# Sample scores in a decoder layer: four transposes and copies first, then four products

## The chip, the cores and the metric

The kernel runs on one core of a Trainium2 chip. The metric is the device time of one execution in microseconds (us), as the median of several. PE is the TensorE engine (matrix products and transposes by a product with the identity), PEld its weight loads, DVE is VectorE, ACT is ScalarE, POOL is GpSimd, and SP issues most DMAs. PE and PEld run side by side. Each engine works through its own queue in a fixed order and waits where an instruction needs something that is not there yet.

## The reference: what matters of it

One layer of a decoder: a projection, sparse attention in three branches beside a state-space layer, an output projection and a feed-forward network, for 1024 prompt tokens and for 8 sample batches of 4 tokens each. The change is in the attention of the samples. Each batch has 32 query rows (4 tokens, 8 heads); the cached keys come from a window of 512 positions and from 2048 paged positions.

```python
full_s = jnp.concatenate([cache_kv_slc[l, page_table].reshape(row_shape), kv_s], axis=1)
win = jnp.concatenate([cache_kv_win[l], kv_w], axis=1)
...
s_s = jnp.einsum('bqgrd,bqgkjd->bqgrkj', qg, k_sel).reshape(bn, nq, N_KV, GQA, n_sel)
p_s = masked_softmax(s_s * scale, key_pos <= q_pos[None, :, None, None, None])
...
s_w = jnp.einsum('bqgrd,bwgd->bqgrw', qg, kv_win[:, :, 0]) * scale
```

## The kernel before

The samples are worked on in two halves of four batches. A half has five runs of 512 cached keys for each batch: one run of the window (branch 2) and four runs of the paged cache (branch 1). Names read `s`, branch, batch, run: `s102kT` are the turned keys of branch 1, batch 0, run 2. The first half has batches 0 to 3, the second 4 to 7.

`sample_scores` (L801) makes the scores of a run for the four batches of a half. For each batch `sample_keys` (L815) does three steps: four transposes on PE of the raw keys `s_raw` into one PSUM bank `kt` (L820; the tag `t` has two banks, so that the third batch needs the bank of the first), a copy of 128x512 numbers from that bank to `kT` in SBUF on ACT (L822), and a product of the 32 query columns `qblk` with `kT` into the batch's 32 rows of the bank `ss` (L823). Before, batch i's product stands in the code between the copy of batch i and the transposes of batch i+1. Then DVE masks the scores to `s_S` (L742, L747), takes their maximum (L752), ACT takes the exponential (L753), and `sample_pv` (L825) turns the weights (`pt`) and multiplies them with the values (L840, tile names that end in `o`, such as `s011o`). Behind that, `sample_load` gathers the rows of the run after next (L404, an indirect DMA that POOL issues); it writes into the buffers which that product has read, so the gather waits for it.

The order of the code is not the order of the queues. The program is built with a scheduler (`schedule_with_timeline_sim=True`) that gives every engine's queue its final order and mixes independent strands. Beside the first half's runs stand the compression of the paged keys (`compress`: `craw` gathered, `cxr` copied on ACT at L487, `ct` transposed at L494, split into `cXh` on ACT and `cXl` on DVE at L498 and L499, products `cp` at L516) and a scan of 128 steps on DVE (`ssm_scan`, L1526 to L1529, four small instructions in a chain for each step). Beside the second half's runs stand the first tiles of the prompt's attention: queries turned (`aqt`, `aqA`, `aqB`), scores `as` (L1195, L1196, L1199), maxima `asm` on DVE (L1203, L1211), exponentials `ap` on ACT (L1212), weights turned (`pt`, L1269) and copied (L1271), values `aso` (L1273), and the rest of the scan. The state-space outputs `Y` (L1601) that need the scan come later.

Of the kernel before, what the change touches and what calls it, by code (L numbers as in the profile page):

```python
# [20 lines left out]
D = 1024  # L21
NT = 8          # tiles of 128 prompt tokens
NK = 8          # tiles of 128 input features
# [5 lines left out]
def shape_constants():  # L29
    """Constants that depend on shapes and positions alone, packed as [128, n] columns."""  # L30
# [27 lines left out]
    # sample rows are (batch in the half, token, group, head in the group)  # L58
# [31 lines left out]
class Kernel:  # L90
# [35 lines left out]
    def psum(self, name, **tags):  # L126
        self.pp = self.open(name, space=PS)
        self.pbufs = tags
        self.tags = "to"
        for t in tags:      # the banks go to the tags in this order  # L130
            self.pp.tile([128, 512 * (2 if t == "s" else 1)], F32, tag=t, name=f"{name}_{t}", bufs=tags[t])
# [23 lines left out]
    def load_constants(self, ea):  # L155
# [26 lines left out]
        nc.vector.tensor_scalar(self.gain_q, self.gain_q, 0.125, None, op0=ALU.mult)     # with the scores' scale  # L182
        # vectors over features, turned to feature-major: b_ada 48, norm_mix_g 8, norm_ffn_g 8, attn_out_g 4, ssm_out_g 4
# [12 lines left out]
    # ---- 1/sqrt(x * a + b), elementwise, on a small tile: a guess from the exponent, scaled by c, and three of Newton's  # L196
    # steps without their factor of -1/2, so that the scale turns c into -2 c^3, three times, and ends at one ----
    def rsqrt(self, x, a, b, name, eng=None, tag="", pool=None, bufs=3):
# [5 lines left out]
        # the guess: the bits of (magic - half of the bits) with c in its exponent and sign  # L204
        V.tensor_scalar(y.bitcast(I32), s.bitcast(I32), -0.5, float(0x5F3759DF) + math.log2(-c) * 2 ** 23 - 2 ** 31, op0=ALU.mult, op1=ALU.add)
        for _ in range(3):
            V.tensor_tensor(t, y, y, op=ALU.mult)
            V.tensor_tensor(t, t, s, op=ALU.mult)
            if eng:     # only the vector engine does both at once
                V.tensor_scalar(t, t, 3.0 * c * c, None, op0=ALU.subtract)  # L210
                V.tensor_tensor(y, t, y, op=ALU.mult)
            else:
                V.scalar_tensor_tensor(y, t, 3.0 * c * c, y, op0=ALU.subtract, op1=ALU.mult)
# [18 lines left out]
    def ada_features(self, nb, ev, out):  # L232
        """out [128 feature, 4, 9] for the four 128-feature blocks, with the bias."""
# [8 lines left out]
    def ada_rows(self, nb, ev, pool, dst):  # L242
        """the nine rows, with the bias, to DRAM."""
# [34 lines left out]
    def phase_project(self):  # L278
        self.psum("psa", s=2, t=3, o=1)
        self.adaT = self.cst.tile([128, 4, 8, 9], F32, name="adaT")   # shift1, (1 + scale1) gain, and the FFN's  # L280
# [92 lines left out]
    def prep_c(self, pa):  # L373
        """silu of the nine conditions, feature-major; they come as rows (row, k-tile) of 128."""
# [26 lines left out]
    def gather(self, out, cache, b, j):  # L401
        """four positions of each of the 128 16-position chunks of a batch's paged rows: [128, 1024]."""
# [4 lines left out]
    def split(self, raw, hi, lo):  # L407
        """raw = hi + lo, each of twelve bits."""
# [3 lines left out]
    def compress_weights(self, pa, pb):  # L412
# [4 lines left out]
        for i, s in enumerate("kv"):  # L417
# [16 lines left out]
            # the encodings' part of the hidden layer: products summed over the positions, then over the partitions  # L434
# [13 lines left out]
    def compress(self, b, cp):  # L448
        """the compressed keys and values of a paged batch (the ninth is the prompt), four positions of each chunk at a
        time; the products of one part follow the turning of the next, and the output's product comes later still."""  # L450
# [23 lines left out]
    def c_turn(self, b, j, cp):  # L474
        """four positions turned and split, two positions times 64 on the partitions: [(hi, lo)] of keys and values."""
# [27 lines left out]
    def c_product(self, b, j, X, cp):  # L503
        """their part of the hidden layer, for the blocks that begin and the blocks that end with the chunk."""
# [51 lines left out]
    def gelu2(self, out, x, t):  # L556
        """twice the tanh form of gelu: x (1 + tanh(sqrt(2 / pi) (x + 0.044715 x^3))); t is scratch."""
# [7 lines left out]
    def sigmoid2(self, out, z):  # L565
        """twice the sigmoid: 1 + tanh(z / 2)."""
# [31 lines left out]
    def sample_modulate(self, xn, out, iscale, ishift, p):  # L598
        """xn [32, 1024] normalised rows to feature-major modulated out [128, 8, 32]."""
# [10 lines left out]
    def sample_qkv(self, ea, sa):  # L610
# [20 lines left out]
        # gates, as rows (b, t, g, r) of three  # L631
# [7 lines left out]
        # queries, block-diagonal over the two groups  # L639
# [22 lines left out]
    def sample_attend(self, half, sb):  # L662
        """a half of the sample batches; rows (batch, token, group, head). The keys come in runs of 512 cached ones
        (the last run of a branch has the new ones behind it), each with its own maximum; the runs are weighed at the end. It goes in seven steps,
        the second half's between the products of the prompt's attention."""
# [7 lines left out]
        # compressed branch  # L673
# [15 lines left out]
        # importance of the 30 blocks that are not forced, the ranks, the mask of those not among the best 13  # L689
# [27 lines left out]
        # the new keys' scores, of both other branches  # L717
# [42 lines left out]
        # weights of the runs: exp(their maximum - the largest) gate / sum; M holds the maxima negated  # L760
# [19 lines left out]
    def sample_begin(self, sb):  # L780
        """the runs of both halves; their rows are loaded two runs ahead."""
# [19 lines left out]
    def sample_scores(self, run, sb):  # L801
        half, br, j = run
        p = self.ps(self.XT[0], f"ss{half}{br}{j}")
        for i, raw in enumerate(self.raws[run]):
            b = 4 * half + i
            self.sample_keys(raw, b, p[32 * i:32 * i + 32, :], sb, i, f"s{br}{b}{j}")
        return p

    def own_group(self, out, O):
        """the own group's half of O [128 row, (g, d)]."""  # L810
# [4 lines left out]
    def sample_keys(self, raw, b, out, sb, i, name):  # L815
        """scores of the batch's 32 rows against four positions of each chunk: out [32, (l, chunk)]."""
# [5 lines left out]
        nc.scalar.copy(kT, p)  # L822
        nc.tensor.matmul(out, self.qblk[:, b, :], kT, start=True, stop=True)  # L823
# [22 lines left out]
    def modulated(self, xn, hi, lo, ishift, iscale, pool, name, tag="mod_h", bufs=2, banks=None, halves=(0, 1)):  # L846
        """normalised rows xn [128, 1024] of one prompt tile (or a half of them) to modulated feature-major hi and lo."""
# [15 lines left out]
    def prompt_rows(self, tt, xp, after=None):  # L863
        """a tile of the prompt, its rows over their root mean square."""
        nc = self.nc
        x = xp.tile([128, 1024], F32, tag="bx", name=f"bx{tt}")
        if after is not None:     # the modulation's weights come first
# [14 lines left out]
    def project_weights(self, nm, col, n, after=None):  # L882
        """n columns of the projection's weights, by halves of the features: as they are, and in high and low parts."""
# [14 lines left out]
    def project(self, cw, first):  # L898
# [9 lines left out]
        if 1:  # L908
            for kind, i, col, n in blocks:
# [7 lines left out]
                for t2 in range(NT // 2):  # L917
# [11 lines left out]
                    if kind == "u":  # L929
                        if nm == "u1" and t2 == 3:      # what follows in place of pb doesn't wait for it  # L930
# [18 lines left out]
            # gates  # L949
# [31 lines left out]
    def kv_turn(self, br, t2, kn, pb):  # L981
        """the keys split, high and low parts stacked over the partitions."""
# [12 lines left out]
    # ---- phase 3: the prompt's attention; between its products the state-space outputs and their gating, the rest of the  # L995
# [893 lines left out]
```

## Time and profile before

| | us |
|---|---|
| median of three executions | 1857.84 |
| the three executions | 1857.84, 1870.40, 1857.72 |
| span of the profiled execution | 1867.2 |
| PE busy in that span | 1779.7 (95%) |
| DVE, ACT, POOL busy | 953.9, 632.4, 423.4 |

The page of the profile tells the span of its execution and not the time around it. Of the three times only 1870.40 lies above that span, by 3.2 us. The other two are 12.6 us shorter than 1870.40.

### The profile page before, as it was taken

How to read it: one execution, taken by the hardware profiler on the slowest of the kernel's cores; microseconds unless marked ns; L12 is line 12 of the kernel's file. 1: busy time of each engine (PE TensorE's matmuls, PEld its weight loads, DVE VectorE, ACT ScalarE, POOL GpSimd, SP SyncE). 2: the span in 40 equal slices, each digit the busy share in tenths (PEclk: the TensorE clock that was granted, in tenths of full speed). 3: DMA queues.
4: the chain of work that ended last, by engine and by line, in shares of the span. 5: the costliest groups of instructions: out<-in, count | busy, mean ns of one | idle time of the engine just before them, and what ended most of it. 6: DMA issues, size and time to landing. Idle time of an engine off the chain costs nothing.

```text
span 1867.2 us, 29377 instructions
## 1 busy us (share of the span) xinstructions
PE 1779.7 (95%) x11546; PEld 1476.4 (79%) x11546; DVE 953.9 (51%) x2330; ACT 632.4 (34%) x1263; POOL 423.4 (23%) x817
## 2 busy tenths in 40 slices
PE   6898999899898999999989989999999999999997
PEld 3788998777655676565658889999999999999996
DVE  4867657667978433655755452332332332332346
ACT  4422146455555342565643341211211211211210
POOL 2334645232025310333112210100100100100140
PEclk9999999999899886999999999999999999999999
DMA  8333244544141111544225331201201201201113
GB/s 290 103 83 111 73 141 125 214 149 157 58 142 66 27 37 31 174 158 155 87 91 178 102 113 46 68 23 46 68 23 46 68 23 46 68 23 46 51 46 139
DMA packets 132700, 172.44 MB, mean 92 GB/s; under 512 B 17177, under 2 KB 92313, under 8 KB 132305
## 3 DMA queue, kind: packets, MB, share of 16 engines
q1 hardware_dynamic: 123024, 136.62, 23.0%
q0 software_dynamic: 9408, 33.89, 5.7%
q8 instruction: 91, 1.49, 0.3%
q14 instruction: 49, 0.39, 0.1%
q10 hardware_dynamic: 128, 0.04, 0.0%
HBM read 143.88 MB, written 25.46 MB: 91 GB/s over the span
## 4 chain that ended last, share of the span: by engine, by line
PE 83%; DVE 8%; DMA 4%; ACT 3%; issue 2%; POOL 0%; SPq 0%; another core or an unknown queue 0%; DVEq 0%; ACTq 0%; POOLq 0%
PE gu L1793 18%; PE dn L1836 13%; PE g L1793 5%; PE u L1793 4%; PE cp L516 4%; PE aso L1273 4%; PE Y L1601 2%; PE as L1195 2%; PE ss L823 1%; PE as L1196 1%; PE q0p L927 1%; PE ct L494 1%; PE q1p L927 1%; PE u1p L927 1%; PE kv0p L927 1%
## 5 line engine op out<-in xcount | busy, mean ns | idle before, releaser
L1793 PE MATMUL gu<-h2h,wh 128*128 128x352 f32 x704 | 227.9, 324 | 5.0 <-ACT h2h L860 5.0
L1793 PE MATMUL gu<-h2h,wl 128*128 128x352 f32 x704 | 227.4, 323 | 0.0
L1793 PE MATMUL gu<-h2l,wh 128*128 128x352 f32 x704 | 226.9, 322 | 0.0
L1842 DVE TENSOR_TENSOR acc<-acc,dn 128x512 f32<-128x512 f32 x144 | 98.8, 686 | 229.6 <-PE dn L1836 229.6
L1801 POOL TENSOR_TENSOR al<-fa,ah 128x352 fp32r<-128x352 f32 (+1 forms) x66 | 69.5, 1053 | 415.1 <-ACT ah L1800 408.8
L1796 ACT ACTIVATE fa<-gu 128x352 f32<-128x352 f32 x44 | 20.4, 465 | 412.5 <-PE gu L1793 412.5
L1836 PE MATMUL dn<-dh,ah 128*128 128x512 f32 x352 | 140.4, 399 | 5.2 <-DVE fin L1845 4.6
L1793 PEld LDWEIGHTS gu<-h2h,wh 128*128 128x128 f32 x704 | 132.6, 188 | 7.9 <-ACT h2h L860 5.3
L1836 PE MATMUL dn<-dl,ah 128*128 128x512 f32 x352 | 138.7, 394 | 0.0
L1836 PE MATMUL dn<-dh,al 128*128 128x512 f32 x352 | 138.3, 393 | 0.0
L1793 PEld LDWEIGHTS gu<-h2l,wh 128*128 128x128 f32 x704 | 133.0, 189 | 3.8
L1793 PEld LDWEIGHTS gu<-h2h,wl 128*128 128x128 f32 x704 | 132.9, 189 | 3.0
L409 ACT CAST wh<-wr 128x1024 fp32r<-128x1024 f32 x44 | 46.0, 1048 | 154.2 <-PE g L1793 77.0
L1799 DVE TENSOR_TENSOR fa<-fa,gu 128x352 f32<-128x352 f32 x44 | 22.9, 521 | 143.8 <-ACT fa L1796 143.8
L1195 PE MATMUL as<-kst,aqA 128*128 128x320 f32 (+4 forms) x192 | 79.7, 420 | 7.0 <-ACT ap L1212 2.9
L1836 PEld LDWEIGHTS dn<-dh,ah 128*128 128x128 f32 x352 | 66.1, 188 | 24.3 <-ACT wh L409 7.5
L410 DVE TENSOR_TENSOR wl<-wr,wh 128x1024 fp32r<-128x1024 f32 x44 | 58.8, 1338 | 49.8 <-ACT wh L409 49.8
L1836 PEld LDWEIGHTS dn<-dl,ah 128*128 128x128 f32 x352 | 66.1, 188 | 15.6
L1836 PEld LDWEIGHTS dn<-dh,al 128*128 128x128 f32 x352 | 66.3, 188 | 8.1
L1211 DVE TENSOR_REDUCE asm<-as 128x1 f32<-128x640 f32 (+3 forms) x64 | 58.7, 921 | 26.1 <-PE as L1199 25.5
L1196 PE MATMUL as<-kst,aqB 128*128 128x320 f32 (+4 forms) x192 | 67.4, 355 | 4.4 <-ACT aqB L1158 4.2
L1212 ACT ACTIVATE ap<-as,asm 128x640 f32<-128x640 f32 (+3 forms) x64 | 55.8, 874 | 27.4 <-DVE asm L1211 17.4
(2135 smaller groups left out, 4735.6 us busy)
## 6 DMA issues: line engine op xcount, KB each, us to landing
wada<-in_w_ada SPq DMA_DIRECT2D x24, 1024.0 KB
wr<-in_w_ffn_gate SPq DMA_DIRECT2D x22, 512.0 KB
wr<-in_w_ffn_up SPq DMA_DIRECT2D x22, 512.0 KB
wd<-in_w_ffn_down SPq DMA_DIRECT2D x22, 512.0 KB
bx<-in_x_prompt SPq DMA_DIRECT2D x8, 512.0 KB
s_raw<-in_cache_kv_win SPq DMA_DIRECT2D x8, 512.0 KB
wor<-in_w_out SPq DMA_DIRECT2D x16, 256.0 KB
ex<-x_d SPq DMA_DIRECT2D x8, 512.0 KB
```

Of the source, the lines that this page charges most:

```text
L410: self.nc.vector.tensor_tensor(lo, raw, hi.bitcast(F32), op=ALU.subtract)
L516: nc.tensor.matmul(P[:, 256 * ab:256 * ab + 256], w[:, 8 * ab + 2 * j + i, :], x[:, i, :], start=j == 0 and i == 0 and n == 0 and ab == 0, ...
L927: nc.tensor.matmul(p[:, t, :n], h[:, k, tok], ww[:, k % 4, :n], start=m == 0, stop=m == 23)
L1195: nc.tensor.matmul(Sv, qA[:, h, :], kk, start=True, stop=False)
L1196: nc.tensor.matmul(Sv, qB[:, h, :], kk, start=False, stop=not mt)
L1211: nc.vector.tensor_reduce(mx[:, :1], Sv, axis=ax, op=ALU.max, negate=True)
L1212: nc.scalar.activation(Pv, Sv, AF.Exp, bias=mx[:, :1], accum_out=l[:, h:h + 1])
L1273: nc.tensor.matmul(O[64 * g:64 * g + 64, 256 * hf:256 * hf + 256], V[:n, 64 * g:64 * g + 64], pT[:, 256 * g:256 * g + 256], start=first, s ...
L1793: nc.tensor.matmul(gu[i], w[:, k, :], h[:, k, 352 * n:352 * n + 352], start=m == 0, stop=m == 23)
L1801: nc.gpsimd.tensor_tensor(al[:, cols], a[:, :w], ah[:, cols].bitcast(F32), op=ALU.subtract)
L1836: nc.tensor.matmul(p, a[:, sl], w[:, c], start=m == 0, stop=m == 5)
L1842: nc.vector.tensor_tensor(o, o, p, op=ALU.add)
```

## The change

In `sample_scores` a first loop turns and copies the keys of all four batches, and a second loop writes the four products one behind the other. `sample_keys` no longer makes the product but returns `kT`. One thing more changes: the copies of batches with an odd place in the half (1 and 3) go to DVE instead of ACT. That is 4 batches x 5 runs x 2 halves = 40 copies, of which 20 move. The rest of the diff takes out comments and docstrings, which moves line numbers: in the changed file the product is L808, the transposes L822, the copies L824, and lines behind them stand two further down.

```diff
     def sample_scores(self, run, sb):
+        nc = self.nc
         half, br, j = run
         p = self.ps(self.XT[0], f"ss{half}{br}{j}")
-        for i, raw in enumerate(self.raws[run]):
-            b = 4 * half + i
-            self.sample_keys(raw, b, p[32 * i:32 * i + 32, :], sb, i, f"s{br}{b}{j}")
+        kT = [self.sample_keys(raw, sb, i, f"s{br}{4 * half + i}{j}") for i, raw in enumerate(self.raws[run])]
+        for i in range(4):
+            nc.tensor.matmul(p[32 * i:32 * i + 32, :], self.qblk[:, 4 * half + i, :], kT[i], start=True, stop=True)
         return p
...
-    def sample_keys(self, raw, b, out, sb, i, name):
+    def sample_keys(self, raw, sb, i, name):
         nc = self.nc
         p = self.ps("t", name + "kt")
         for l in range(4):
             nc.tensor.transpose(p[:, 128 * l:128 * l + 128], raw[:, l, :128], self.ident)
         kT = sb.tile([128, 512], F32, tag="s_kT", name=name + "kT", bufs=4)
-        nc.scalar.copy(kT, p)
-        nc.tensor.matmul(out, self.qblk[:, b, :], kT, start=True, stop=True)
+        (nc.vector.tensor_copy if i % 2 else nc.scalar.copy)(kT, p)
+        return kT
```

The scheduler makes a new order of all queues in the stretch of both halves. The order of the program's instructions differs from rows 1977 to 2976 of 9073 on PE; before and behind that it is the same. Counted over the whole PE queue, the 40 products stand in 31 unbroken rows of one to four products before, and in 29 such rows now (20 to 19 in the first half, 11 to 10 in the second). Three places:

First, PE in run 2 of the first half, before:

```order
L823 MATMUL ss_5504<-s112kT,qblk 32x512
L820 MATMUL s132kt<-ident,s_raw_2_5498 128x128 x4
L494 MATMUL ct_01_6306<-ident,cxr_0_6295 128x128 x4
L516 MATMUL cp_6167<-cXh_30_6256,w1lk 128x256
L516 MATMUL cp_6167<-cXh_30_6256,w1hk 128x256
L516 MATMUL cp_6167<-cXl_30_6257,w1hk 128x256
L516 MATMUL cp_6167<-cXh_30_6256,w1lk 128x256
L516 MATMUL cp_6168<-cXh_31_6265,w1hv 128x256
L823 MATMUL ss_5504<-s122kT,qblk 32x512
```

and the same products on PE after the change:

```order
L822 MATMUL s132kt<-ident,s_raw_2_5498 128x128 x4
L808 MATMUL ss_5504<-s112kT,qblk 32x512
L516 MATMUL cp_6168<-cXl_21_6212,w1hv 128x256
L516 MATMUL cp_6168<-cXh_21_6211,w1lv 128x256
L516 MATMUL cp_6168<-cXh_21_6211,w1hv 128x256
L516 MATMUL cp_6168<-cXl_21_6212,w1hv 128x256
L494 MATMUL ct_31_6260<-ident,cxr_3_6249 128x128 x2
L808 MATMUL ss_5504<-s122kT,qblk 32x512
```

The four transposes of batch 3 now stand ahead of batch 1's product, but products of the compression still lie between the scores' products.

Second, PE at the first transposes of run 3 of the first half, before:

```order
L516 MATMUL cp_6380<-cXl_11_6376,w1hv 128x256
L516 MATMUL cp_6380<-cXh_11_6375,w1lv 128x256
L516 MATMUL cp_6380<-cXh_11_6375,w1hv 128x256
L516 MATMUL cp_6380<-cXl_11_6376,w1hv 128x256
L820 MATMUL s103kt<-ident,s_raw_3_5563 128x128 x4
```

and after:

```order
L516 MATMUL cp_6379<-cXh_00_6302,w1lk 128x256
L516 MATMUL cp_6379<-cXh_00_6302,w1hk 128x256
L516 MATMUL cp_6379<-cXl_00_6303,w1hk 128x256
L516 MATMUL cp_6379<-cXh_00_6302,w1lk 128x256
L494 MATMUL ct_11_6370<-ident,cxr_1_6359 128x128 x4
L822 MATMUL s103kt<-ident,s_raw_3_5563 128x128 x4
```

The last row of `s011o`, behind which the gather of these keys begins, stands 44 rows ahead of `s103kt` before and 28 rows ahead of it now: 24 products `cp` and three groups of transposes `ct` are left between them. Between `s010o` and `s102kt`, the same place of run 2, 38 `cp` and three groups `ct` stand now.

Third, DVE from the masking of the second half's last scores on, before:

```order
L747 TENSOR_TENSOR s_S_7647<-ss_7614,s_neg_6855 128x512
L1529 TENSOR_TENSOR ssm_H<-ssm_H,scan_123_4968 128x32
L1203 TENSOR_REDUCE asm_7871<-as_7870 128x2
L752 TENSOR_REDUCE s_M_6874<-s_S_7647 128x1
L1271 COPY ac4pT_7776<-ac4pt_7777 64x512
L1526 TENSOR_TENSOR scan_124_4974<-ssm_LA,ssm_H 128x32
```

and after:

```order
L747 TENSOR_TENSOR s_S_7647<-ss_7614,s_neg_6855 128x512
L1261 TENSOR_SCALAR acl_7831<-acl_7831,kc 128x8
L1531 TENSOR_TENSOR ssm_H<-ssm_H,scan_118_4938 128x32
L1205 TENSOR_REDUCE asm_7883<-as_7882 128x2
L1273 COPY ac4pT_7776<-ac4pt_7777 64x512
L752 TENSOR_REDUCE s_M_6874<-s_S_7647 128x1
L1528 TENSOR_TENSOR scan_119_4944<-ssm_LA,ssm_H 128x32
```

The scan is five steps further back at the same place: from here to the first maximum of the next tile (`asm_7939`, L1211) DVE has 70 rows in place of 50. At the start of the second half it is the other way round: between the compressed scores' maximum (`cm`, L681) and the first `asm` of the prompt's attention there are 13 rows of the scan in place of 23, and the copies of `s250kT` and `s270kT` are new there.

On POOL the gather of `craw_2` (the compression's third piece of batch 7) now stands behind the four gathers of run 2 instead of ahead of them, and the clearing of `craw_1` behind the four gathers of run 3. SP's queue has the same order as before.

## Rows read from the trace of the kernel before

**Rows 1.** Busy time of each engine (and instructions) by stage, granted clock:

```profile
core 0: us, PE busy (x) PEld busy (x) DVE busy (x) ACT busy (x) POOL busy (x), PEclk, DMA share, GB/s
340.00:476.00 136.00, 128.06 (x1026) 101.66 (x1025) 97.86 (x443) 71.38 (x138) 34.58 (x35) 0.97 0.49 167
476.00:580.00 104.00, 92.92 (x740) 61.71 (x739) 85.56 (x336) 56.65 (x138) 15.22 (x20) 0.93 0.24 78
...
640.00:760.00 120.00, 119.05 (x812) 83.20 (x810) 51.80 (x106) 48.97 (x114) 12.79 (x34) 0.82 0.18 50
...
480.00:500.00 20.00, 16.06 (x96) 12.22 (x97) 18.82 (x65) 9.40 (x20) 0.00 (x0) 0.77 0.09 27
```

**Rows 2.** PE's instructions in order of time: a product alone (start, us):

```profile
364.62 1.05 PE L823 MATMUL ss<-s200kT,qblk 128*32 128x512 f32 x2
365.60 0.44 PE L820 MATMUL s220kt<-ident,s_raw 128*128 128x128 f32 x2
```

**Rows 3.** PE in order of time: four products in a row, second half, run 0:

```profile
515.80 0.62 PE L823 MATMUL ss<-s140kT,qblk 128*32 128x512 f32 x1
...
515.82 0.62 PE L823 MATMUL ss<-s170kT,qblk 128*32 128x512 f32 x1
...
516.79 0.66 PE L1269 MATMUL as401pt<-ident,ap 128*128 128x128 f32 x4
```

**Rows 4.** PE in order of time around the gather of run 3:

```profile
432.76 1.08 PE L840 MATMUL s011o<-s_raw,s011pT 128*32 128x128 f32 x32
...
434.11 0.28 PE L516 MATMUL cp<-cXh,w1lk 128*128 128x256 f32 x1
434.23 0.29 PE L516 MATMUL cp<-cXh,w1hk 128*128 128x256 f32 x1
...
436.99 0.60 PE L494 MATMUL ct<-ident,cxr 128*128 128x128 f32 x4
437.35 0.36 PE L516 MATMUL cp<-cXl,w1hk 128*128 128x256 f32 x1
...
440.72 0.66 PE L820 MATMUL s103kt<-ident,s_raw 128*128 128x128 f32 x4 [0.91 <-DMA s_raw<-in_cache_kv_slc,idx]
```

**Rows 5.** PE in order of time: the same distance for run 2:

```profile
411.14 1.08 PE L840 MATMUL s010o<-s_raw,s010pT 128*32 128x128 f32 x32
...
418.64 0.60 PE L820 MATMUL s102kt<-ident,s_raw 128*128 128x128 f32 x4
```

**Rows 6.** Gathers of run 2 on POOL, and the copy of `craw_2` on ACT:

```profile
412.48 0.94 POOL L404 DMA_INDIRECT s_raw<-in_cache_kv_slc,idx  x1 [1.21 <-PE s010o L840]
413.72 0.94 POOL L404 DMA_INDIRECT s_raw<-in_cache_kv_slc,idx  x1 [0.30 <-issue]
...
433.39 1.06 ACT L487 COPY cxr<-craw 128x1024 f32<-128x1024 f32 x1
```

**Rows 7.** A copy of 128x512 on ACT (L822) and one on DVE (L1271):

```profile
L822 ACT COPY s200kT<-s200kt x1: 586/586/586, 361.7 to 361.7; 128x512 f32<-128x512 f32 x1
577.78 0.68 DVE L1271 COPY as000pT<-as000pt 128x512 f32<-128x512 f32 x1
```

**Rows 8.** Who waited for the copies of L822 (us, times):

```profile
  PEld s260kt L820: 0.2, 1
```

**Rows 9.** Longest waits of PE, 476 to 620 us (total, times, longest):

```profile
PE as L1196 <- ACT aqB L1158: 3.3, 3, 1.3
PE as L1195 <- ACT ap L1212: 2.8, 4, 1.9
```

**Rows 10.** DVE in order of time, the end of the scan's stretch:

```profile
570.23 0.69 DVE L747 TENSOR_TENSOR s_S<-ss,s_neg 128x512 f32<-128x512 f32 x1 [0.28 <-PE ss L823]
...
574.10 0.18 DVE L1526 TENSOR_TENSOR scan<-ssm_LA,ssm_H 128x32 f32<-128x32 f32 x1
574.20 0.19 DVE L1527 TENSOR_TENSOR scan<-ssm_LA,ssm_H 128x32 f32<-128x32 f32 x1
...
587.40 1.08 DVE L1211 TENSOR_REDUCE asm<-as 128x1 f32<-128x896 f32 x1
```

## The prediction

> **What bounds the kernel now.** I read the stages first. The change touches only two of them, which together are 240 us of 1867: the first half with the compression (340 to 476 us) and the second half with the first tiles of the prompt's attention (476 to 580 us). In the first PE is busy 128.1 of 136 us, in the second 92.9 of 104 us [rows 1]. So PE is the bound, and all that a perfect order could win back there is its idle time, 7.9 + 11.1 = 19.0 us. DVE is second with 97.9 and 85.6 us. It is full at one place, 480 to 500 us, with 18.8 of 20 us, and there PE falls to 16.1 us and the granted clock to 0.77, between the two levels of 1.2 and 2.4 GHz [rows 1]. ACT has room in both stages (71.4 of 136, 56.7 of 104 us). What shortens the kernel is therefore fewer PE microseconds or fewer PE waits. Time taken off ACT counts only where PE waits for ACT, and time put on DVE counts where DVE is what PE waits for.
>
> A product alone takes PE from 364.62 to 365.60, 0.98 us [rows 2]. Four that stand in a row start within 0.02 us, each pass of each in its own 32 columns, and the next instruction starts at 516.79: 0.99 us for all four [rows 3]. So the cost is counted in unbroken rows of products, not in products.
>
> **Products put together.** The title of the change suggests 10 rows for the 10 runs. The order of the PE queue says otherwise: 31 rows before, 29 now, because the scheduler still puts other work between them. 2 x 0.98 = 2.0 us less on PE. The bounds are 0, if a gap opens in place of the product, and 2.1, by the longer duration of 1.05 in the row. I take **-2.0 us**, since PE is the bound in both stages.
>
> **Transposes that come earlier than their keys.** To bring the products forward the scheduler has also pulled transposes forward, towards the gather that fills their buffer. In the trace `s011o` ends at 432.76 + 1.08 = 433.84 and the transposes of run 3 start at 440.72, after a wait of 0.91 us for the DMA [rows 4]: the keys are there 6.9 us behind the product that frees the buffer. Now 24 products `cp` and three groups `ct` lie between. A `cp` takes 434.23 - 434.11 = 0.12 us and a group 437.35 - 436.99 = 0.36 us [rows 4], so 2.9 + 1.1 = 4.0 us of work covers 6.9 us, and the wait is 2.9 in place of 0.9: +2.0 us. For run 2 the distance before is 418.64 - 412.22 = 6.4 us without a wait [rows 5]. Now 38 `cp` and three `ct` stand there, 4.6 + 1.1 = 5.7 us. The wait is 0 if that gather is quicker, 0.7 if the keys came just in time, 1.2 if they take 6.9 us too. I take 0.7, by its own rows. Together **+2.7 us**, with bounds 0 and 3.2.
>
> **Gathers moved on POOL.** `craw_2` is now issued behind four gathers 1.24 us apart that begin at about 412.48, so at 417.4; with the 6.9 us from above it is there by 424.3. The copy that needs it runs at 433.39 [rows 6], so 9 us of other work hide the move, and the clearing of `craw_1` has its use later still. Cost nothing; if the cover were gone, the four gathers' 5.0 us.
>
> **Twenty copies from ACT to DVE.** The ACT copy takes 0.59 us and a DVE copy of the same shape 0.68 us [rows 7], so ACT loses 11.8 us and DVE gains 13.6 us. On ACT's side, nobody waited for one of these copies longer than 0.2 us [rows 8]: the two banks already hide them, and I take 0. The other waits of PE for ACT, 3.3 us for `aqB` and 2.8 us for `ap` [rows 9], are not caused by the copies in any row, but their sum of 6.1 us bounds a gain. The Trainium skill, on the page TensorEngine Tiling (Array Packing), section PSUM Bottleneck, advises to empty PSUM with ScalarE and VectorE together once the products are packed. By that rule the copies would go in half the time, and the sum would fall by at most the 11.8 us; the 0.2 us of these rows says that there is almost nothing to win here.
>
> On DVE's side, ten copies fall into the first half, where DVE has 38 us idle, and eight into 500 to 580 us; 18 x 0.68 = 12.2 us. I take 0, as idle DVE time covers it: 38 us in the first stage, 18 us in the second [rows 1]. Queued behind a DVE copy that waits for its transposes are the scan and the low parts `cXl`, for which PE waits in turn, so without that cover all 12.2 us would show.
>
> **The two places where DVE leads.** At the start of the second half DVE gets two copies, 1.4 us, but ten fewer rows of the scan ahead of the first maximum. In a full DVE queue scan rows start 0.10 us apart and take 0.18 us [rows 10], so that is 1.0 to 1.8 us less: between -0.4 and +0.4, and I take 0. The postponed scan comes back at the end. From `s_S` at 570.23 to the first maximum of the next tile at 587.40 [rows 10] DVE ran almost without a gap and now has 20 more rows: 20 x 0.10 = 2.0 us, at most 20 x 0.18 = 3.6, and 0 if the copies' time is found before it. I take **+2.0 us**, by the start-to-start distance, which is what a full queue pays.
>
> **The sum** is -2.0 + 2.7 + 0 + 2.0 = +2.7 us. Against the profiled span that is 1867.2 + 2.7 = 1869.9 us; against the median, 1857.84 + 2.7 = **1860.5 us**. The profiled span is 9.4 us above the median. The stage behind the change, 640 to 760 us, has PE busy 119.1 of 120 us at a mean clock of 0.82 [rows 1]; if 36% of it ran at 1.2 GHz, 43 us did, and 22 us of that are lost. That place could hold the 12.6 us between the executions, but one trace can't show it.
>
> **The rivals.**
> *The products do go together* (the change does what it says in full): 21 rows fewer than 31, 21 x 0.98 = 20.6 us, 1837.3 us. The four products in 0.99 us speak for its price [rows 3], the order with 29 rows against it. The page TensorE: Matmul & The Clock Gate of the Trainium skill, in Part 3 on packing small matmuls, has n products in separate columns take the time of one plus some 4 ns for each further one; the trace agrees with 0.02 us over four, and it is the rule on which such a gain rests. 3%.
> *ACT's relief pays*: the 6.1 us of waits for ACT go [rows 9], the 2.0 us of products too, and nothing comes back: 1849.7 us. For it: those waits are PE's longest in that stage. Against it: `aqB` waits for its transposes and DVE as well, not for a key copy. 12%.
> *DVE becomes the bound of the second half* (slower): its ten copies there show in full, 6.8 us, with the 2.7 us of DMA and the 2.0 us at the end, less 2.0: +9.5. PE then waits more, as at 480 to 500 us, where a clock of 0.77 means 9.2 of 20 us at 1.2 GHz and 4.6 us lost [rows 1]; one more such stretch makes +14.1, 1871.9 us. It decides when the copies land where DVE has no gap: DVE's 18.4 us idle in the second stage must be reached by 6.8 us of copies at the right moments. 15%.
> *The typical execution is the longer one*: 1860.5 + 12.6 = 1873.1 us, from the clock alone. 8%.
> *The forecast*, a small change of either sign around the sum: 62%.
>
> **How the numbers follow.** The likeliest case gives 1860.5. The range runs from 1849 (ACT's relief) to 1872 (DVE as the bound). It leaves out the first rival, the last, and a little of the forecast's own spread. About 1%, 18.6 us, is what a measurement of this kernel tells from no change. Faster by that needs the first rival, 3%. Slower by that needs the last two rivals together or a wait that I have not seen, 6%. Within 1%: 91%.
>
> **What would show it.** In the changed kernel's profile: products (L808) in rows of one in the first half, each still near 0.98 us; a wait for the DMA of some 2.9 us ahead of `s103kt`; DVE busy 13 to 14 us more over 340 to 600 us and ACT 12 us less; the scan's last step later; the first `asm` of the second half no later than before. The prediction is wrong if PE's idle time in the two stages grows by more than 10 us, if the waits for `aqB` vanish with the ACT copies, or if the clock behind 600 us settles at another level.

## The result and the profile after

The changed kernel takes 1875.16 us (median of five executions, 1872.77 to 1879.39) against 1858.66 us for the kernel before (median of five): ratio 1.0079, 95% interval 1.0052 to 1.0105. The forecast of 1860.5 us and its range up to 1872 us were both too low. The loss of some 14.7 us (0.0079 x 1859) is well outside the uncertainty, though below the 1% that the chances spoke of.

The two profiled spans hide this: 1871.0 us after against 1867.2 us before. The traced execution of the kernel before was a long one. It reached the first transposes of the change (`s200kt`) at 360.4 us, the changed kernel at 354.1 us, although the programs are the same up to there. For the comparison of stages I therefore use a second profile of the kernel before (the experiment "before again" below, span 1862.2 us), and count from marks that both programs have, not from absolute time. That execution (1863.93 us) is the longest of its eleven and the changed kernel's profiled one the shortest of its five, so the windows below can understate the loss.

The stages of [rows 1] in the changed kernel, at the same absolute times (busy time of each engine, granted clock):

```profile
core 0: us, PE busy (x) PEld busy (x) DVE busy (x) ACT busy (x) POOL busy (x), PEclk, DMA share, GB/s
340.00:476.00 136.00, 125.99 (x1018) 101.13 (x1017) 103.73 (x450) 68.12 (x131) 32.22 (x34) 0.99 0.49 170
476.00:580.00 104.00, 92.05 (x745) 60.72 (x745) 89.36 (x341) 50.19 (x127) 17.69 (x27) 0.93 0.24 76
640.00:760.00 120.00, 119.28 (x823) 83.43 (x821) 51.38 (x108) 45.93 (x109) 11.86 (x33) 0.79 0.15 40
```

DVE is busier by 5.9 and 3.8 us than in [rows 1], ACT idler by 3.3 and 6.5 us. In these absolute times the two programs stand some 6 us apart; cut at the marks below, DVE gains 4.0 and 3.6 us in the two halves and ACT loses 5.2 and 5.1, as the copies ask. PE's idle time in the two stages is 10.0 + 12.0 us, 2.9 us more than before. Nothing here says 15 us. The marks do. The next windows of the changed kernel run from `s200kt` to the start of the products of run 1 with the values (`s011o`, behind which the gathers of run 3 are issued), to the first transposes of the second half (`s240kt`), to the start of the last such products of the sample tokens (`s113o`), to the first `aco` of tile 0 (weights of the compressed branch times values), and to the first `hpo` (`ssm_H` turned on PE):

```profile
354.14:421.78 67.64, 66.65 (x505) 50.62 (x503) 48.63 (x188) 34.21 (x63) 16.98 (x18) 1.00 0.42 140
421.78:478.19 56.41, 48.51 (x432) 41.04 (x432) 43.55 (x206) 26.26 (x52) 10.49 (x11) 0.97 0.44 147
478.19:573.69 95.50, 85.99 (x673) 56.86 (x670) 81.20 (x304) 47.10 (x119) 13.05 (x14) 0.93 0.24 75
573.69:597.29 23.60, 17.54 (x120) 11.40 (x120) 19.94 (x47) 10.11 (x20) 17.37 (x27) 0.78 0.33 119
597.29:748.26 150.97, 149.34 (x1005) 105.27 (x1005) 63.86 (x129) 53.27 (x130) 31.92 (x51) 0.79 0.12 30
```

The same five windows of the kernel before, in its second profile:

```profile
358.53:429.41 70.88, 70.68 (x529) 53.14 (x527) 50.33 (x210) 41.21 (x77) 17.97 (x19) 1.00 0.43 140
429.41:476.74 47.33, 43.67 (x408) 36.64 (x408) 37.85 (x183) 24.44 (x49) 9.87 (x10) 1.00 0.47 165
476.74:572.35 95.61, 88.79 (x674) 59.72 (x670) 77.60 (x301) 52.21 (x126) 13.13 (x14) 0.91 0.23 75
572.35:590.71 18.36, 14.96 (x121) 9.83 (x120) 16.85 (x32) 10.58 (x23) 16.58 (x27) 0.91 0.38 139
590.71:739.53 148.82, 147.19 (x1004) 103.97 (x1004) 63.95 (x129) 53.37 (x130) 32.58 (x51) 0.82 0.13 33
```

Three places make the difference. The first half (first two windows) takes 124.0 us against 118.2: +5.8. The second half is the same, 95.5 against 95.6. The **start of the next tile**, 23.6 against 18.4 us, loses 5.2. The long stage behind it loses 2.1, at a clock of 0.79 against 0.82 with PE busy 99% in both. Together +13.1 us of the 14.7.

**First half.** PE around the gather of run 3, which answers to [rows 4]:

```profile
421.78 1.08 PE L842 MATMUL s011o<-s_raw,s011pT 128*32 128x128 f32 x32
...
427.53 0.66 PE L822 MATMUL s103kt<-ident,s_raw 128*128 128x128 f32 x4 [0.34 <-DMA s_raw<-in_cache_kv_slc,idx]
...
432.20 0.66 PE L822 MATMUL s113kt<-ident,s_raw 128*128 128x128 f32 x4 [2.46 <-DMA s_raw<-in_cache_kv_slc,idx]
...
435.32 1.05 PE L808 MATMUL ss<-s103kT,qblk 128*32 128x512 f32 x2
```

The predicted wait for the gather is there, 2.5 us at `s113kt` and not 2.9 at `s103kt`. The waits of PE in the first half show what else is new:

```profile
PE s113kt L822 <- DMA s_raw<-in_cache_kv_slc,idx: 2.5, 1, 2.5
PE cw L548 <- DVE ssm_H L1531: 1.6, 1, 1.6
PE cw L543 <- DVE scan L1530: 1.6, 1, 1.6
PE s121kt L822 <- DMA s_raw<-in_cache_kv_slc,idx: 1.0, 1, 1.0
PE cw L552 <- DVE ssm_H L1531: 0.9, 1, 0.9
PE ct L494 <- DVE cXl L499: 0.9, 1, 0.9
```

Gathers cost 3.8 us here (0.4 in before again). Waits that end with a DVE row are 5.0 us; before again has 2.8 us of them, so 2.2 are new: a product of the compression (L543) stands behind the scan, another group behind the low parts `cXl`. PE's idle time rose from 3.9 to 8.9 us; that explains 5.0 of the 5.8.

**Start of the next tile.** DVE in order of time, which answers to [rows 10] (the changed kernel):

```profile
580.30 1.21 DVE L1528 TENSOR_TENSOR scan<-ssm_LA,ssm_H 128x32 f32<-128x32 f32 x1
581.42 0.18 DVE L1529 TENSOR_TENSOR scan<-ssm_LA,ssm_H 128x32 f32<-128x32 f32 x1
581.63 0.68 DVE L1159 CAST aqB<-aqt 64x512 fp32r<-64x512 f32 x1
...
582.96 1.49 DVE L1541 TENSOR_TENSOR ssm_hs<-ssm_hs,ssm_Hs 128x128 f32<-128x128 f32 x1
...
585.08 1.30 DVE L1367 TENSOR_TENSOR ssm_hs<-ssm_ts,ssm_ts 128x128 f32<-128x128 f32 x1
586.30 1.20 DVE L1531 TENSOR_TENSOR ssm_H<-ssm_H,scan 128x32 f32<-128x32 f32 x1
587.42 1.08 DVE L1213 TENSOR_REDUCE asm<-as 128x1 f32<-128x896 f32 x1
```

POOL in the same microseconds:

```profile
580.21 1.24 POOL L1362 TENSOR_TENSOR Ctt<-ssm_par 128x576 f32<-128x576 f32 x1
...
582.84 1.46 POOL L1364 TENSOR_TENSOR Ct<-Ctt,Ctt 128x576 f32<-128x576 f32 x1
...
586.19 1.26 POOL L1366 TENSOR_TENSOR Ctt<-ssm_par 128x576 f32<-128x576 f32 x1
```

The two scan rows that take 1.2 us instead of the 0.18 of [rows 10] start 0.1 us behind a product of POOL and end within 0.1 us of its end: 580.30 + 1.21 = 581.51 beside 580.21 + 1.24 = 581.45, and 587.50 beside 587.45. The Trainium skill, page SBUF — State Buffer, section SBUF: two separate sides, says that of a DVE operation with two inputs in SBUF and a GpSimd operation that reads SBUF, the one that starts first holds a shared pair of ports for its whole instruction, and that the other one waits; the trace agrees, with these ends. At `s113o` five steps of the scan are still to do, where before again has one. The other eighteen scan rows behind `s113o` take 0.17 to 0.19 us. The first maximum `asm` starts 587.42 - 573.69 = 13.7 us behind `s113o`; in before again it is 10.8 us:

```profile
583.11 1.08 DVE L1213 TENSOR_REDUCE asm<-as 128x1 f32<-128x896 f32 x1
```

PE waits for what follows the maximum, in before again 0.74 us, in the changed kernel 3.41 us in one piece (the longest `ap` wait in [rows 9] is 1.9). The first line is of before again, the others of the changed kernel:

```profile
585.38 0.50 PE L1197 MATMUL as<-kst,aqA 128*128 128x512 f32 x1 [0.74 <-ACT ap L1214]
...
589.68 0.80 PE L1197 MATMUL as<-kst,aqA 128*128 128x512 f32 x1 [3.41 <-ACT ap L1214]
...
596.21 0.50 PE L1197 MATMUL as<-kst,aqA 128*128 128x512 f32 x1
```

The same instruction takes 0.80 us there and 0.50 us at 596.21: PE runs at the lower clock around the wait. Over this window 0.22 x 23.6 = 5.2 us are lost to the clock; before again loses 0.09 x 18.4 = 1.7. The lost clock is not simply added to the time here. The first profile of the kernel before takes as long at full clock:

```profile
576.62:595.01 18.39, 13.46 (x120) 8.62 (x119) 16.87 (x32) 10.59 (x23) 16.61 (x27) 1.00 0.38 139
```

Of the 5.2 us by which the window is longer, 3.0 lie ahead of the first maximum, and 2.3 behind it: 597.29 - 587.42 = 9.9 us against 590.71 - 583.11 = 7.6.

**The clock over a whole execution.** Each execution comes with its span and its mean granted clock, so the time lost to the clock can be worked out as span x (1 - clock), and the rest as span x clock. The changed kernel: 64.8 us lost and 1809.0 rest (mean of five); the kernel before, 23 executions beside the first experiments: 48.7 lost and 1808.8 rest. By these means nearly all of the loss is booked to the clock, but the five were not run beside the 23. Where the changed kernel was run beside the kernel before (changed again, below), the clock has 10.7 of 13.3 us. In the five windows above it has some 8 of the 13.1 (1.7 + 6.7 + 5.2 + 31.7 = 45.3 us lost against 8.6 + 1.7 + 26.8 = 37.1). That does not make the clock the cause (waits change which stretches run low), but it says where most of the loss is booked.

### The profile page after: what moved, and what is told of

Same layout as the page of the kernel before. It is cut to its first block, busy times and chain, and to the rows that moved or that the text cites. A ratio compares the mean times of both kernels' runs of the same rounds, so it can differ in the third digit from the quotient of the medians.

```text
span 1871.0 us, 29370 instructions
## 1 busy us (share of the span) xinstructions
PE 1779.3 (95%) x11546; PEld 1478.3 (79%) x11546; DVE 965.0 (52%) x2350; ACT 621.9 (33%) x1243; POOL 422.1 (23%) x817
## 4 chain that ended last, share of the span: by engine, by line
PE 84%; DVE 8%; DMA 4%; ACT 2%; issue 1%; POOL 0%; SPq 0%; DVEq 0%; ACTq 0%; POOLq 0%
PE gu L1795 18%; PE dn L1838 13%; PE u L1795 5%; PE g L1795 5%; PE cp L516 4%; PE aso L1275 4%; PE Y L1603 2%; PE as L1197 2%; PE ss L808 2%; PE as L1198 1%; PE ct L494 1%; PE q0p L929 1%; PE kv1p L929 1%; PE q1p L929 1%; PE u1p L929 1%
## 5 line engine op out<-in xcount | busy, mean ns | idle before, releaser
L1798 ACT ACTIVATE fa<-gu 128x352 f32<-128x352 f32 x44 | 20.4, 464 | 412.4 <-PE gu L1795 412.4
```

## The experiments

All ratios are to executions of the kernel before on the same chip beside them: median 1859.0 us for the first four, 1859.9 for the next four, 1866.5 for the last four, each group on a chip of its own. The table has each kernel's profile cut at the marks from above (us). One profile is not exact to a microsecond: the first half of the changed kernel takes 124.0 us in one and 125.8 in the other.

| kernel | ratio [95%] | first half | second half | tile start | behind it |
|---|---|---|---|---|---|
| before again | 0.9993 [0.9984, 1.0002] | 118.2 | 95.6 | 18.4 | 148.8 |
| changed | 1.0079 [1.0052, 1.0105] | 124.0 | 95.5 | 23.6 | 151.0 |
| changed again | 1.0074 [1.0058, 1.0090] | 125.8 | 95.5 | 23.6 | 150.9 |
| order only | 1.0026 [1.0011, 1.0041] | 115.6 | 96.9 | 18.3 | 146.0 |
| copies only | 1.0074 [1.0050, 1.0099] | 119.1 | 97.8 | 25.1 | 151.2 |
| first half only | 1.0099 [1.0067, 1.0131] | 123.8 | 98.1 | 24.1 | 150.8 |
| second half only | 1.0026 [1.0010, 1.0042] | 119.6 | 95.4 | 19.5 | 150.7 |
| order, copies in the second half | 0.9992 [0.9975, 1.0008] | 115.7 | 90.0 | 20.4 | 148.5 |
| reversed (from `s230kt` and `s270kt`, its first transposes) | 1.0086 [1.0068, 1.0105] | 127.8 | 99.1 | 19.6 | 147.5 |
| scan short | 1.0059 [1.0042, 1.0076] | 127.3 | 97.3 | 19.6 | 147.3 |
| other keys | 1.0085 [1.0062, 1.0108] | 121.8 | 98.3 | 21.9 | 150.0 |
| keys and scan | 1.0030 [1.0019, 1.0041] | 121.7 | 97.3 | 19.5 | 147.2 |
| before, scan short | 1.0019 [1.0007, 1.0030] | 119.7 | 94.9 | 18.3 | 152.0 |

**Order only.**

```diff
-        (nc.vector.tensor_copy if i % 2 else nc.scalar.copy)(kT, p)
+        nc.scalar.copy(kT, p)
```

> The changed kernel with all twenty copies back on ACT: only the order is changed, keys of four batches first, then four products (again 29 unbroken rows of products against 31). Copies theory (what is lost is DVE's 20 copies of 0.68 us, which come late for the maxima and the scan): ratio to the kernel before 0.998 to 1.002. Order theory (transposes and products in their new places wait for gathers, DVE and each other): ratio 1.006 to 1.010, as the whole change has 1.0079. Reshuffle theory (any change of the order loses what the old order had found): 1.003 to 1.006.

It came between the theories, at 1.0026, about a third of the changed kernel's loss. Its first half is even shorter than before, 115.6 against 118.2 us, with 0.6 us of waits for `s_raw`: between `s011o` and `s103kt` its trace has 40 products `cp`, as against 41 before and 24 in the changed kernel. So the run's transposes do not move towards their gather by the new order of the code alone, but where the copies of the first half are on DVE too.

**Copies only.**

```diff
-        kT = [self.sample_keys(...) for i, raw in enumerate(self.raws[run])]
-        for i in range(4):
-            nc.tensor.matmul(p[32 * i:32 * i + 32, :], self.qblk[:, 4 * half + i, :], kT[i], ...)
+        for i, raw in enumerate(self.raws[run]):
+            kT = self.sample_keys(...)
+            nc.tensor.matmul(p[32 * i:32 * i + 32, :], self.qblk[:, 4 * half + i, :], kT, ...)
```

> The order of the kernel before (each batch's product behind its own copy), with the copies of the odd batches on DVE. 31 unbroken rows of products as before. Copies theory: ratio 1.006 to 1.010, with the late wait for the exponentials ap (3.4 us at 586 to 590 us in the changed kernel) and the clock under 0.8 in 580 to 600 us. Order theory: 0.998 to 1.002. Reshuffle theory: 1.003 to 1.006.

1.0074, the copies theory's number. Its first half is only 0.9 us longer than before. Of the 12.2 us that its four columns have more, 9.1 lie behind `s113o`, 6.7 of them in the window of the next tile's start, with DVE busy 23.1 of 25.1 us and a clock of 0.80:

```profile
572.29:597.40 25.11, 16.25 (x119) 10.23 (x120) 23.08 (x58) 10.12 (x21) 17.53 (x27) 0.80 0.31 112
```

**First half and second half alone.** The new order and the copies are used where `half == 0`, or where `half == 1`, and the old ones elsewhere:

```diff
+        if half == 0:
             kT = [...]
...
-        (nc.vector.tensor_copy if i % 2 else nc.scalar.copy)(kT, p)
+        (nc.vector.tensor_copy if i % 2 and half == 0 else nc.scalar.copy)(kT, p)
```

> The change in the first half of the batches alone (ten copies on DVE, keys first); the second half is built as before. Copies theory with DVE as bound in the second half: 0.999 to 1.002, since DVE has room in the first half. Order theory: most of the loss, 1.004 to 1.008, as the waits for the gather (2.5 us) and for the scan (4.1 us) lie at 420 to 480 us. Reshuffle theory: 1.003 to 1.006.

> The change in the second half alone; the first is built as before. Copies theory with DVE as bound in the second half: 1.004 to 1.009, with a stall and half clock at 575 to 600 us. Order theory: 0.999 to 1.003. Reshuffle theory: 1.003 to 1.006.

The first half alone costs as much as the whole change, 1.0099; the second alone 1.0026, which only the order theory's range held. So the copies theory as I had it, with the second half's copies as the burden, is refuted, and with it the place that my rival on the slower side named. The burden is the first half's. Yet its cost at the tile start is paid 100 us later: 24.1 us there, with all copies of the second half back on ACT.

**The changed kernel and the kernel before again.** No edit in the first; in the second both parts are undone, which gives the order of before on all engines.

> The changed kernel itself once more, for a second profile of it and beside more executions of the kernel before. In the executions so far its span times its mean granted clock is the same as the kernel before's (1809.0 against 1808.8 us), and only the time lost to the clock differs (64.8 against 48.7 us). Clock theory (the loss is in the granted clock, and part of it sits at fixed places): ratio 1.006 to 1.010, lost time 12 to 18 us above the kernel before's in the same runs, and the half clock behind 580 us stands in this profile too. If the place was chance: the same ratio, but 580 to 600 us at full clock here.

> Both parts undone in the changed kernel's text, which gives the kernel before's order of instructions on every engine. It says how far a ratio of two identical programs strays, and gives a second profile of that program. All theories: 0.999 to 1.001. If the profile of before was one of its long executions, this one has a span of 1853 to 1862 us, and less than 57.9 us lost to the clock.

The loss repeats (1.0074), identical programs agree within 0.1% (before again has the span of 1862.2 us at the end of the range that was expected, and 52.4 us lost), and the tile start is not chance: 23.6 us and a clock of 0.78 in both profiles of the changed kernel. Lost to the clock here: 61.2 us on average against 50.5 us, 10.7 more, with 2.6 us more of the rest (1810.7 against 1808.1).

**Reversed.** The kernel before with the batches taken from the last to the first:

```diff
-        for i, raw in enumerate(self.raws[run]):
+        for i, raw in reversed(list(enumerate(self.raws[run]))):
```

> The kernel before with the four batches of a run gone through from the last to the first: the same instructions on the same engines, each product behind its own copy, all copies on ACT; only the order differs (32 unbroken rows of products against 31). Reshuffle theory (each new order of the queues loses some 5 us of clock, as the order alone and the second half alone did with 1.0026 each): 1.002 to 1.004. If those 5 us belong to the keys being ahead of the products: 0.999 to 1.001.

Both expectations missed: 1.0086, without one copy on DVE. It is no neutral reshuffle. The gathers are still issued from the first batch to the last, so the first transposes now want the keys that come last. PE's longest wait in its first half:

```profile
PE s132kt L822 <- DMA s_raw<-in_cache_kv_slc,idx: 3.7, 1, 3.7
```

Its first half takes 127.8 us against 118.2, and its tile start is short. Two new waits for DVE rows (L541 and L543, 2.7 us together) stand beside the 4.0 us for `s_raw`, so the gathers are not shown to be all of it. It shows that an order alone can cost as much as the change, at the other one of the two places.

**Order in both halves, DVE copies in the second alone.**

```diff
-        (nc.vector.tensor_copy if i % 2 else nc.scalar.copy)(kT, p)
+        (nc.vector.tensor_copy if i % 2 and half == 1 else nc.scalar.copy)(kT, p)
```

> The changed order in both halves, DVE copies in the second half alone, the first half's copies all on ACT. It has 24 unbroken rows of products against 31, so 6.9 us less of them on PE by 0.98 us each. First-half theory (ten DVE copies of the first half hold up the scan and the low parts; the second half's don't): 1.000 to 1.004. Copies theory (any ten on DVE cost half of the change's loss): 1.004 to 1.007. If packed products pay: 0.996 to 0.999.

0.9992, between the ranges of the first-half theory and of packed products: with the first half's ten copies on ACT the loss is gone, and so are most waits for `s_raw` (0.9 us in the first half; 40 `cp` again between `s011o` and `s103kt`). This kernel has the fewest rows of products, 24 against 31. Span x clock is 1802.1 us on average against 1808.1, 6.0 us less, which fits the 6.9 us of seven products at 0.98; other differences of the order are not told apart from it. But 54.9 us are lost to the clock against 50.5, which gives 4.4 of them back. It is the best form of the change, and no faster than the kernel before.

**The two places taken away.** First the steps of the scan that are left over, then the wait for the gather, then both; and the first edit in the kernel before.

```diff
-        for c in range(128):
+        for c in range(123):
```

> The changed kernel without the last five of the scan's 128 steps (20 rows of DVE are left out, and with them the last states); the order on PE, ACT and POOL is word for word the changed kernel's. In the changed kernel five steps are still to do when the last product of the sample tokens (s113o) starts, in the kernel before one; the first maximum of the next tile starts 13.7 us behind s113o against 10.8, and s113o to the first aco of ac0 takes 23.6 us against 18.4. Scan theory (the steps left over meet POOL's matrices, where a row takes 1.2 us in place of 0.18, and stand ahead of the maximum): first maximum at 10.7 to 11.5 us, the stretch 18.3 to 20 us, ratio down from 1.0077 to 1.003 to 1.006. Rival, chance of the clock (the stretch is long since the clock falls there by itself): the stretch stays at 22 to 24 us and the ratio at 1.006 to 1.009.

In the window the scan theory holds: the first maximum starts 10.8 us behind `s113o`, and the tile start takes 19.6 us at a clock of 0.91. The stage behind it is 3.7 us shorter than the changed kernel's:

```profile
581.89:601.52 19.63, 14.84 (x120) 9.50 (x119) 15.81 (x27) 10.30 (x22) 16.36 (x27) 0.91 0.41 143
601.52:748.81 147.29, 145.66 (x1006) 102.67 (x1005) 63.73 (x129) 53.34 (x130) 32.33 (x51) 0.83 0.13 31
```

With the order of PE, ACT and POOL unchanged, twenty rows of DVE are worth 23.6 - 19.6 = 4.0 us at the tile start. That the 3.7 us behind it come from them too is not shown: the kernel before with the same rows left out takes 152.0 us there, behind a tile start of 18.3. The ratio is 1.0059 against 1.0077, the mean of the changed kernel's two; the intervals overlap, and the changed kernel was not run on this chip, so the ratio alone doesn't show the gain. This profile's first half is longer, 127.3 us, with 0.10 x 59.9 = 6.0 us lost to the clock there.

```diff
+        if half == 0 and (br, j) == (1, 3):
+            raws = [raws[0], raws[0], raws[2], raws[3]]
```

> The changed kernel with the keys of batch 1 of run 3, first half, read from batch 0's tile (its scores there are batch 0's keys; its own gather is still done and its values are used), so that its transposes don't wait for their gather. POOL's order stays, PE's changes in some 28 rows. Gather theory (the 2.5 us wait of s113kt for its gather is lost time of PE): s200kt to s240kt falls from 124.0 and 125.8 us to 120 to 122.5, ratio from 1.0077 to 1.005 to 1.007. Rival, the wait is only moved (to s123kt, or to the products of the compression that wait for DVE): 123.5 to 126 us, ratio 1.007 to 1.009.

The first half falls to 121.8 us, as the gather theory says, and the wait of `s113kt` is gone. The ratio of 1.0085 is a miss, in the range of the rival: the second half takes 98.3 us here, and the tile start keeps 21.9 us.

> Both of the last two edits: no wait for that gather, and five steps of the scan left out. If these two places are what the change costs: 1.000 to 1.004. If the loss is a matter of the clock behind 600 us alone, whatever stands ahead: 1.005 to 1.009.

> The kernel before without the last five steps of the scan (the same rows left out as in the changed kernel's). It says what leaving these rows out is worth by itself. Scan theory: the kernel before has only one step left over, so 0.997 to 1.000. If leaving out scan rows shortens every kernel: 0.994 to 0.997, as much as it gives the changed one.

Together 1.0030, as expected if these two places are what the change costs, with an interval below both of the changed kernel's. The kernel before with the same rows left out came to 1.0019, a miss: it is not below 1.000, and why it is slower is not known (on average it has 2.4 us more of lost clock and 1.6 us more of the rest). Leaving out scan rows is worth nothing by itself. Against that kernel 1.0030 - 1.0019 = 0.0011 remain of the change's 0.0077, about 2 us, which the two intervals don't tell from nothing.

The scan left over at `s113o` can be followed through other kernels. In copies only 33 of its rows stand behind `s113o`, six of them of 0.9 to 1.5 us, and the tile start takes 25.1 us. In the changed kernel there are 20, two of them of 1.2 us, and 23.6 us; with copies in the second half alone 16, one of 1.2 us, and 20.4 us; in before again 4, all short, and 18.4 us.

## Why the prediction was wrong

**Products together, -2.0.** Right in kind. A product alone still takes its microsecond (1.05 us in its row), and the kernel with 24 rows has 6.0 us less of span x clock, where the price gives 6.9. It was never the term that decides.

**Transposes closer to their gathers, +2.7.** The size came out, in part by luck: 3.8 us of waits for `s_raw` in the first half, 0.9 in [rows 4] and 0.4 in before again. But the keys of `s103kt` were there 427.53 - 422.86 = 4.7 us behind `s011o`, not 6.9, and that wait was 0.3 us; the 2.5 us stand at the next batch, and run 2 has none. The reason was wrong too: it was not the products brought forward that pulled these transposes ahead, for in the kernels with the new order and the first half's copies on ACT 40 `cp` lie there and not 24.

**POOL's moves, 0, and the start of the second half, 0.** Right: no row waits for `craw`, the first maximum stands 8.8 us behind `s240kt` against 10.7, and the second half takes the same time.

**Twenty copies, 0: the step that failed.** I took ten copies of the first half as free "as idle DVE time covers it: 38 us". A share of idle time is no cover for a chain that runs through the whole stretch in small steps. With copies queued between its steps the scan fell behind: counted in the trace, 85 steps are still to do at `s011o` against 79 in before again, and five against one at `s113o`. I had named the scan and `cXl` as what queues behind a copy, and let the 38 us answer for it. The new waits for DVE in the first half, 2.2 us, are the smaller part of the bill. In place of 0 the twenty copies cost 0.0074 x 1859 = 13.8 us in the old order of the code (copies only), and the first half's ten are the difference between 1.0077 and 0.9992 in the new one, some 16 us with the rows of products that the scheduler then packs.

**The postponed scan, +2.0: mis-sized by the same error.** I priced 20 more rows at 0.10 to 0.18 us, from a stretch where POOL was quiet. The last of them landed where POOL has its matrices to do, and two took 1.2 us each. The first maximum came 3.0 us later, which the bound of 3.6 held. But no term stood for what the stall does next: behind the maximum the tile start is 2.3 us longer, with PE's rows at the lower clock there, and the stage behind it is 2.1 us longer. The rival "DVE becomes the bound" had part of this mechanism, with 4.6 us for one more stretch at the lower clock and 1871.9 us in all, which is 3 us from the measured median. I put it into the second half's copies, and judged it by that stage's idle time; the first and second half alone show that it is the first half's copies, and that much of the bill comes where the chain ends.

**The typical execution.** I feared that the profile of before might be the normal one. Twenty-three executions have a median of 1859.9 us: it was the traced one that was long.

**The signs I gave.** None of the three by which I would have known the failure came clearly: PE's idle time in the two stages grew by 2.9 us, not 10, the waits for `aqB` are 4.5 us, and the clock behind 640 us is 0.79 against 0.82. They watched the stages of the change and not the one behind it, where the chain ends.

**What stays open.** The first half alone also has a tile start of 24.1 us, but its scan ends 2.6 us behind `s113o`, as in before again (2.4). There other DVE rows of 1.3 to 1.7 us (L1371, L1372, the split of `aqhl`) stand ahead of the second `aqB` and of the first maximum. So the place is DVE's queue beside POOL's matrices; which rows are in it depends on the order. Whether the ten copies act by their time or by the order that the scheduler makes around them was not separated. What the traces do show is that the scan falls behind wherever they are on DVE: at `s011o` 79 of the 128 steps are left in all kernels that take the batches from first to last with these copies on ACT, 82 in copies only, 85 in the changed kernel and in first half only. Nor is it settled why the stage behind 600 us loses 22 to 33 us to the clock from one kernel to the next with PE busy 99%.

## What to carry to other kernels

Idle time of an engine doesn't cover new work if a long chain of small dependent steps runs on it: look up where that chain ends, what then waits behind it, and price its last steps there, beside what other engines do at that moment. Look behind a stall too, for here PE's rows ran at the lower clock after it; span x mean clock beside span x (1 - clock), over several executions, shows which of the two a change has moved. Work that an off-path engine does for nothing (ACT's copies, here) is not worth moving, and transposes should keep the order in which their gathers are issued.

## What the runs showed of the hardware

A DVE row of 128x32 with both inputs in SBUF takes 0.18 us alone and 1.20 to 1.21 us when POOL's product of 128x576 has started 0.1 us ahead of it. The kernel before loses 46 to 60 us of an execution to the clock in 23 executions on one chip, the changed one 54 to 66 in six; the largest share of it in a stage where PE has hardly a gap (149.3 of 151.0 us busy at a clock of 0.79). In the changed kernel the keys of the second of four gathers, issued 1.25 us apart, could be used 432.20 - 424.37 = 7.8 us behind its issue on POOL; those of the first 427.53 - 423.12 = 4.4 us behind theirs.
